# Token-stationary gate sums and projections in a hybrid diffusion trunk layer

## Chip, core and metric

The kernel runs on one core of one Trainium2 chip. The time is device microseconds of one execution, as the median of several runs. TensorE (PE) multiplies, VectorE (DVE) and ScalarE (ACT) do elementwise work, SyncE (SP) issues most transfers. Each of these works through its own queue in order, and a wait at the head holds what is behind it.

## What is computed

One trunk layer is applied to 128 context tokens and 256 latent tokens, 384 tokens in all (`TOK`), with `D_MODEL` 2048. Everything is float32. The part that matters here is `token_mixing`, between the input projection and the feed-forward part:

```python
def token_mixing(h, attn, u, w_na_proj, w_fnet_proj, w_gate, w_o):
    b, t = h.shape[:2]
    na = attn.reshape(b, t, D_NA) @ w_na_proj
    fn = fourier_mix(u) @ w_fnet_proj
    g_na, g_fn = jnp.split(jax.nn.sigmoid(h @ w_gate), 2, axis=-1)
    return (g_na * na + g_fn * fn) @ w_o
...
x = x + g1 * token_mixing(h, attn, u, ...)
h2 = rms_norm(x, n2) * (1 + sc2) + sh2
x = x + g2 * swiglu(h2, w_gu_l, w_down_l)
```

`h` is the normed and modulated input, `attn` the attention's output (1024 wide), `fourier_mix(u)` the real part of a 2-D DFT (1024 wide). `w_gate` is 2048 x 4096, the two projections 1024 x 2048 each, `w_o` 2048 x 2048.

## The kernel before

**Products.** A float32 product is made of three matmuls in a reduced format, `mm3` (L146 to L149): each operand is split into a high part H, cast by ScalarE (L143), and a low part L, the rest, by VectorE (L144). The first two operands of `mm3` (aH, aL) stand in the array as stationary operand, the last two (bH, bL) move through it. The stationary operand is 128 x 128; the moving one here has 384 or 512 columns. So there are two ways to do a product. With the tokens standing and 512 weight columns moving, the result has tokens on the partitions; w_in, w_o and w_down are done so (3 blocks of 128 tokens x 2 rows of the contraction x 3 = 18 matmuls a unit). With a 128 x 128 block of weights standing and 384 tokens moving, the result has channels on the partitions, as the next product's contraction needs them; the gate sums, the projections and w_gate_up are done so (4 blocks of 128 columns x 2 x 3 = 24 matmuls a unit).

**Weights.** All weights pass in units of 256 rows x 512 columns, in one list (`units`): w_in, w_gate (64 units), the two projections in turns of four units (32), w_o (32), then the feed-forward weights. A unit is loaded on SP's queue (L187) into one of four `wraw` buffers, split into one of three `wh` and `wl` buffers by `split_unit`, and used. `next_unit` sets the order: it splits a unit two ahead of the one it hands out, then gives each background piece its steps, then issues the next load.

**Background pieces.** A background piece is a Python generator that a `Paced` object advances by so many steps for each unit; each step puts instructions into the queues behind what is there already. `rows` adds up the modulation rows of the second norm and the gates (VectorE, L329, loads on SP, L299) at about one step a unit. During the gate sums a second one, `branches`, holds the Fourier mix and then the attention, with steps at the head of a unit and once in its middle (`mid_unit`).

**Gate sums.** For each of eight column blocks of w_gate (`fc8`), eight units of matmuls add into four PSUM tiles of 128 channels x 384 tokens. They are copied out (`gst`, L1033) by VectorE or ScalarE and stored to DRAM (`s_gate`, L1036) by ScalarE's queue.

**Projections and mix.** For each of four column blocks (`f4`), the stored gates are loaded (`load_gates`, three tiles `gl`), the sigmoid is taken, and four units of w_fnet_proj and then four of w_na_proj are multiplied; each result is multiplied into its gate tile (L1094). The mix of the block (`mixed`) is a background piece with two steps a unit: add the two gated parts (L1069), split the sum into `mixH` and `mixL`, which lie channels first, as w_o's contraction wants them. After the last block, everything in the background but `rows` is drained at once, and w_o begins (`for cc in range(4)`, L1168 on): tokens standing, sixteen k-tiles of the mix, residual and gain added at the end of each `cc`.

Of the kernel before, what the change touches and what calls it, by code (L numbers as in the profile page):

```python
# [13 lines left out]
F32 = mybir.dt.float32  # L14
# [5 lines left out]
P = 128  # L20
D = 2048
KT = D // P
# [7 lines left out]
TOK = CTX + LAT  # L30
NT = TOK // P
EPS = 1e-6
CH = 512
# [19 lines left out]
def fr(ap):  # L53

    return ap.bitcast(F32)
# [46 lines left out]
def trunk_kernel(ctx: ExitStack, tc: tile.TileContext, io: dict):  # L102
    nc = tc.nc
# [27 lines left out]
    dram = ctx.enter_context(tc.tile_pool(name="dram", bufs=1, space=DRAM))  # L131
# [6 lines left out]
    def nm(s):  # L138
        return f"{s}{next(ids)}"


    def split(H, L, x):
        nc.scalar.copy(H, x)  # L143
        nc.vector.tensor_sub(L, x, fr(H))  # L144

    def mm3(out, aH, aL, bH, bL, start, stop):  # L146
        nc.tensor.matmul(out, aH, bH, start=start, stop=False)  # L147
        nc.tensor.matmul(out, aH, bL, start=False, stop=False)  # L148
        nc.tensor.matmul(out, aL, bH, start=False, stop=stop)  # L149
# [45 lines left out]
    def split_unit():  # L195
        if loads.got:
            _, raw = loads.take()
            H = wpool.tile([P, 2, CH], F32R, tag="wh", name=nm("wh"))
            L = wpool.tile([P, 2, CH], F32R, tag="wl", name=nm("wl"))
            n = raw.shape[1]  # L200
            split(H[:, :n], L[:, :n], raw)
            ready.append((H, L))

    def mid_unit():
        for p in front:
            p.tick()

    def next_unit():

        for p in front:  # L210
            p.tick()
        split_unit()
        for p in front + behind:
            p.tick()
        loads.more()
        return ready.popleft()
# [12 lines left out]
    hH = [None] * KT  # L229
    hL = [None] * KT  # L230

    def new_h(kt):
        hH[kt] = hpool.tile([P, TOK], F32R, tag=f"tH{kt}", name=nm(f"hH{kt}_"))
        hL[kt] = hpool.tile([P, TOK], F32R, tag=f"tL{kt}", name=nm(f"hL{kt}_"))
        return hH[kt], hL[kt]

    s_qkvu = [dram.tile([P, NT, CH], F32, tag=f"sq{i}", name=f"s_qkvu{i}") for i in range(8)]
    s_gate = [dram.tile([P, 4, TOK], F32, tag=f"sg{i}", name=f"s_gate{i}") for i in range(8)]
    s_row = {
        ty: [dram.tile([1, D], F32, tag=f"row{ty}{c}", name=f"s_row{ty}{c}") for c in range(2)] for ty in (2, 3, 4, 5)  # L240
    }
# [24 lines left out]
    with ExitStack() as ph:  # L266
# [3 lines left out]
        def mm_tile():  # L270
            return ps.tile([P, CH], F32, tag="mm", name=nm("mm"))
# [6 lines left out]
        def new_ring(n=0):  # L278

            nonlocal ring  # L280
            ring = itertools.cycle([mm_tile] * n + [at_tile] * 3 + [mm_tile] * (4 - n))

        def acc_tile():

            return next(ring)()
# [152 lines left out]
        with ExitStack() as pha:  # L438
# [4 lines left out]
            def c6(shape, name):  # L443
                return cpool.tile(shape, F32, tag="c6", name=nm(name))
# [8 lines left out]
            for cc in range(4):  # L453
                t = c6([P, NT, CH], "xc")
# [195 lines left out]
            for gi, (k0, n) in enumerate(GROUPS):  # L650
# [5 lines left out]
                for rate, ci in zip(CHUNKS, ORDER):  # L656
                    if gi == len(GROUPS) - 1:
                        rows.rate = rate
                    po = [(mm_tile if gi < len(GROUPS) - 1 else acc_tile)() for _ in range(NT)]
                    if gi == 0:  # L660
                        acc[ci] = c6([P, NT, CH], "acc")
                    for u in range(k0, k0 + n, 2):
                        wH, wL = next_unit()
                        while prepared[0] < min(u + 2, k0 + n):
                            prep.step()
                        for t in range(NT):
                            sl = slice(t * P, (t + 1) * P)
# [5 lines left out]
                            if u + 2 >= k0 + n:  # L673
                                a = acc[ci][:, t]
# [15 lines left out]
        gst = ph.enter_context(tc.tile_pool(name="gst", bufs=4))  # L690
# [126 lines left out]
        soft = deque(maxlen=3)  # L817
# [197 lines left out]
        front += [br_work, rows]  # L1015
        behind.remove(rows)
        for fc8 in range(8):
            po = [mm_tile() for _ in range(4)]
            sts = []
            for u in range(0, KT, 2):  # L1020
                ending[0] = u == KT - 2
                rows.least = 3 if ending[0] else 1
                wH, wL = next_unit()
                for f in range(4):
                    s = slice(f * P, (f + 1) * P)
                    if f == 2:
                        mid_unit()
                    for kk in range(2):
                        k = u + kk
                        mm3(po[f][:, :TOK], wH[:, kk, s], wL[:, kk, s], hH[k], hL[k], k == 0, k == KT - 1)  # L1030
                    if u == KT - 2:
                        st = gst.tile([P, TOK], F32, tag="st", name=nm("gst"))
                        (nc.vector.tensor_copy if f < 2 and any(soft) else nc.scalar.copy)(st, po[f][:, :TOK])  # L1033
                        sts.append(st)
            for f, st in enumerate(sts):
                nc.scalar.dma_start(s_gate[fc8][:, f], st)  # L1036
        br_work.drain()
        rows.least = 1
        front.clear()
# [4 lines left out]
        bs = ph.enter_context(tc.tile_pool(name="bsplit", bufs=1))  # L1044
# [8 lines left out]
                yield  # L1053

        def load_gates(f4, i):
            g = bs.tile([P, 4, TOK], F32, tag="gl", bufs=3, name=nm("gl"))
            nc.sync.dma_start(g, s_gate[i * 4 + f4])
            return g

# [2 lines left out]
        gates = Ahead(load_gates, [(f4, i) for f4 in range(4) for i in (1, 0)], 3)  # L1062
        mixH, mixL = [None] * KT, [None] * KT

        def mixed(f4, gl):
            for f in range(4):
                kt = f4 * 4 + f
                mixH[kt], mixL[kt] = new_h(kt)
                nc.vector.tensor_add(gl[0][:, f], gl[0][:, f], gl[1][:, f])  # L1069
                split(mixH[kt], mixL[kt], gl[0][:, f])  # L1070
                if f == 3:
                    yield
                    gates.more()
                    gates.more()
                yield

        new_ring(1)
        for f4 in range(4):
            gl = [None, None]
            for i, bH, bL in ((1, fH, fL), (0, aH, aL)):  # L1080
                _, gl[i] = gates.take()
                po = [acc_tile() for _ in range(4)]
                for u in range(0, 8, 2):
                    wH, wL = next_unit()
                    if u == 4:
                        nc.scalar.activation(out=gl[i], in_=gl[i], func=AF.Sigmoid)
                    for f in range(4):
                        s = slice(f * P, (f + 1) * P)
                        for kk in range(2):
                            k = u + kk  # L1090
                            mm3(po[f][:, :TOK], wH[:, kk, s], wL[:, kk, s], bH[k], bL[k], k == 0, k == 7)
                        if u < 6:
                            continue
                        nc.vector.tensor_mul(gl[i][:, f], gl[i][:, f], po[f][:, :TOK])  # L1094
            behind.append(Paced(mixed(f4, gl), 2))
        behind.remove(rows)
        for p in behind:
            p.drain()
# [69 lines left out]
    for cc in range(4):  # L1168
        xin[cc] = tmp.tile([P, NT, CH], F32, tag="xin", name=nm("xin"))
        behind.append(Paced(load_residual(cc)))  # L1170
        po = [acc_tile() for _ in range(NT)]
        for u in range(0, KT, 2):
            if cc == 3 and u == KT - 4:
                rows.rate = 0
            if cc == 3 and u == 8:
                warm_sqrt()
            wH, wL = next_unit()
            if cc == 3 and u == KT - 2:
                rows_until(3)
                shifts(xw, 0)  # L1180
            if u == 2 and cc:
                rows_until(4)
                behind.append(Paced(transposed(cc - 1), 0.5))
            for t in range(NT):
                sl = slice(t * P, (t + 1) * P)
                for kk in range(2):
                    k = u + kk
                    mm3(po[t], mixH[k][:, sl], mixL[k][:, sl], wH[:, kk], wL[:, kk], k == 0, k == KT - 1)
                if u == KT - 2:
                    d = tmp.tile([P, CH], F32, tag="d", name=nm("d"))  # L1190
                    nc.vector.tensor_mul(d, po[t], gb[cc][:, min(t, 1)])
                    nc.vector.tensor_add(x2[cc][:, t], xin[cc][:, t], d)
                    junk = tmpo.tile([P, CH], F32, tag="junk", name=nm("junk"))
                    nc.scalar.activation(
                        out=junk, in_=x2[cc][:, t], func=AF.Square, accum_out=ssx[:, t, cc : cc + 1]
                    )
# [96 lines left out]
    for part, nf in enumerate(FF_PARTS):  # L1293
# [5 lines left out]
        for c4 in range(nf // 4):  # L1299
            for half in (1, 0):  # L1300
                po = [acc_tile() for _ in range(4)]
                bs = []
                for u in range(0, KT, 2):
                    wH, wL = next_unit()
                    for f in range(4):
                        s = slice(f * P, (f + 1) * P)
                        for kk in range(2):
                            k = u + kk
# [6 lines left out]
                        if half and f == 0:  # L1315
                            sg = tmp.tile([P, 4, TOK], F32, tag="xin", name=nm("sg"))
# [20 lines left out]
        for cc in range(4):  # L1337
            po = [acc_tile() for _ in range(NT)]
            for u in range(0, nf, 2):
                wH, wL = next_unit()  # L1340
                for t in range(NT):
                    sl = slice(t * P, (t + 1) * P)
                    for kk in range(2):
                        k = u + kk
# [66 lines left out]
```

## Time and profile before

| | |
|---|---|
| median of three runs | 2045.47 us (2044.15 to 2046.48) |
| profiled execution, span | 2046.3 us |
| PE busy | 2023.5 us, 99% |
| weight loads into PE (PEld) | 1843.5 us, 90% |
| VectorE busy | 1260.9 us, 62% |
| ScalarE busy | 741.1 us, 36% |
| gate sums, first to last load of w_gate | 314.9 to 640.1 us |
| projections, first to last load | 643.6 to 782.9 us |
| w_o, first to last load | 789.0 to 916.9 us |

The span is from the first to the last instruction of the profiled execution; the profile gives no separate time for what lies around it. Busy time of an engine is the union of its instructions, whose durations overlap on TensorE, so a TensorE that shows as fully busy says little of how close its matmuls follow each other; the starts in the timeline say that. L12 is line 12 of the kernel. In a group, "out<-in" names what is written and read, then the number of instructions, their busy time and mean ns, and the idle time ahead of them with what ended it. DMA issues have the time from issue to landing. Loads are issued some units ahead of use, so the stretches in the table are those of the loads.

### The profile page before, as it was taken

What the parts mean: (1) busy time and instruction counts of PE and PEld (TensorE: products, weight loads), DVE (VectorE), ACT (ScalarE), POOL (GpSimd) and SP (SyncE); (2) the same over time, 40 slices, a digit from 0 to 9 for tenths busy, and PEclk for the clock granted to TensorE, in tenths of its full rate; (3) what the DMA queues carried; (4) which work ended last, traced back from release to release, by engine and by line L of the source; (5) the groups of instructions that cost most, each with busy time, mean ns of one, the idle gap of its engine ahead of it and who ended that gap; (6) DMA issues with size and microseconds to landing.
All of it is one profiled execution on the core that took longest, in us unless ns stands there. A gap on an engine that the chain in (4) does not pass through costs nothing.

```text
span 2046.3 us, 27564 instructions
## 1 busy us (share of the span) xinstructions
PE 2023.5 (99%) x10986; PEld 1843.5 (90%) x10986; DVE 1260.9 (62%) x1578; ACT 741.1 (36%) x1093; POOL 43.7 (2%) x92
## 2 busy tenths in 40 slices
PE   7999999999999999999999999999999999999999
PEld 4668888999999999889998999899989998999897
DVE  4646989789988778755845454545454334333456
ACT  4433232445555443334523332322322232323222
POOL 1000000000010000010000000000000000000000
PEclk8999999999999999999999999999999999999999
DMA  9995979677775776754455555554554444444453
GB/s 309 335 343 187 321 258 324 217 232 224 231 204 177 250 253 190 247 182 144 119 174 156 153 155 156 150 157 146 160 158 138 124 130 125 132 124 124 138 161 124
DMA packets 220384, 390.46 MB, mean 191 GB/s; under 512 B 28464, under 2 KB 77632, under 8 KB 220256
## 3 DMA queue, kind: packets, MB, share of 16 engines
q1 hardware_dynamic: 213088, 382.13, 59.7%
q10 hardware_dynamic: 4672, 6.31, 0.8%
q8 instruction: 86, 1.41, 0.3%
q0 software_dynamic: 2496, 0.27, 0.1%
q14 instruction: 42, 0.34, 0.0%
HBM read 371.81 MB, written 20.51 MB: 192 GB/s over the span
## 4 chain that ended last, share of the span: by engine, by line
PE 96%; DMA 2%; DVE 1%; ACT 0%; SPq 0%; issue 0%; DVEq 0%
PE mm L147 20%; PE mm L149 19%; PE mm L148 19%; PE at L147 11%; PE at L149 11%; PE at L148 11%; PE at L405 1%; DMA wm<-in_w_mod 1%; DMA wraw<-in_w_in 1%; PE at L978 1%; PE at L957 1%; DMA xc<-in_x_prompt 1%; PE at L894 1%; DVE wl L144 0%; PE at L338 0%; PE at L1154 0%
## 5 line engine op out<-in xcount | busy, mean ns | idle before, releaser
L144 DVE TENSOR_TENSOR wl<-wraw,wh 128x1024 fp32r<-128x1024 f32 (+1 forms) x464 | 559.3, 1206 | 683.8 <-ACT wh L143 683.6
L143 ACT CAST wh<-wraw 128x1024 fp32r<-128x1024 f32 (+1 forms) x464 | 481.1, 1038 | 1086.9 <-PE at L148 273.9
L147 PE MATMUL mm<-hH,wh 128*128 128x384 f32 x1152 | 387.7, 337 | 0.0
L149 PE MATMUL mm<-hH,wl 128*128 128x384 f32 x1152 | 385.2, 334 | 0.0
L148 PE MATMUL mm<-hL,wh 128*128 128x384 f32 x1152 | 385.1, 334 | 0.0
L329 DVE SCALAR_TENSOR_TENSOR accr<-wmr,csz,accr 128x1024 f32<-128x1024 f32 x240 | 304.2, 1280 | 0.1
L147 PEld LDWEIGHTS mm<-hH,wh 128*128 128x128 f32 x1152 | 216.2, 188 | 3.7 <-issue 3.7
L148 PEld LDWEIGHTS mm<-hL,wh 128*128 128x128 f32 x1152 | 216.3, 188 | 0.0
L149 PEld LDWEIGHTS mm<-hH,wl 128*128 128x128 f32 x1152 | 216.2, 188 | 0.0
L147 PE MATMUL at<-hH,wh 128*128 128x384 f32 x640 | 213.9, 334 | 0.0
L149 PE MATMUL at<-hH,wl 128*128 128x384 f32 x640 | 213.9, 334 | 0.0
L148 PE MATMUL at<-hL,wh 128*128 128x384 f32 x640 | 213.8, 334 | 0.0
L147 PE MATMUL mm<-wh,hH 128*128 128x512 f32 x404 | 160.8, 398 | 1.9 <-ACT hH L546 1.2
L148 PE MATMUL mm<-wl,hH 128*128 128x512 f32 x404 | 158.2, 392 | 0.8 <-DVE wl L144 0.8
L149 PE MATMUL mm<-wh,hL 128*128 128x512 f32 x404 | 158.5, 392 | 0.4 <-DVE hL L144 0.4
L147 PE MATMUL mm<-wh,cH 128*128 128x512 f32 x352 | 137.0, 389 | 0.0
L149 PE MATMUL mm<-wh,cL 128*128 128x512 f32 x352 | 137.0, 389 | 0.0
L148 PE MATMUL mm<-wl,cH 128*128 128x512 f32 x352 | 137.0, 389 | 0.0
L147 PEld LDWEIGHTS at<-hH,wh 128*128 128x128 f32 x640 | 120.1, 188 | 1.0 <-ACT wh L143 0.8
L148 PEld LDWEIGHTS at<-hL,wh 128*128 128x128 f32 x640 | 120.1, 188 | 0.2
L149 PEld LDWEIGHTS at<-hH,wl 128*128 128x128 f32 x640 | 120.1, 188 | 0.0
L147 PEld LDWEIGHTS mm<-wh,hH 128*128 128x128 f32 x404 | 76.2, 189 | 26.1 <-issue 4.4
(284 smaller groups left out, 2627.9 us busy)
## 6 DMA issues: line engine op xcount, KB each, us to landing
wraw<-in_w_gate_up SPq DMA_DIRECT2D x176, 512.0 KB, 3.7
wmr<-in_w_mod SPq DMA_DIRECT2D x128, 512.0 KB, 5.0
wraw<-in_w_down SPq DMA_DIRECT2D x88, 512.0 KB, 3.7
wraw<-in_w_gate SPq DMA_DIRECT2D x64, 512.0 KB, 4.6
wm<-in_w_mod SPq DMA_DIRECT2D x80, 384.0 KB, 6.8
wraw<-in_w_in SPq DMA_DIRECT2D x56, 512.0 KB, 5.9
wraw<-in_w_o SPq DMA_DIRECT2D x32, 512.0 KB, 4.7
wraw<-in_w_fnet_proj SPq DMA_DIRECT2D x16, 512.0 KB, 4.8
```

The source lines that it names most:

```text
L143: nc.scalar.copy(H, x)
L144: nc.vector.tensor_sub(L, x, fr(H))
L147: nc.tensor.matmul(out, aH, bH, start=start, stop=False)
L148: nc.tensor.matmul(out, aH, bL, start=False, stop=False)
L149: nc.tensor.matmul(out, aL, bH, start=False, stop=stop)
L329: nc.vector.scalar_tensor_tensor(out=acc[:, cnd], in0=wm, scalar=sc, in1=acc[:, cnd], op0=ALU.mult, op1=ALU.add)
L405: nc.tensor.matmul(pm[q : q + 32, :w], csz[:, k, :], wm[:, ty, kk + par, :], start=k < 2, stop=k >= KT - 2, tile_position=(0, q), skip_gro ...
L894: nc.tensor.matmul(po[j][:, cols], qx[rows[j], q], kx[rows[j], k], start=i == 0, stop=i == 2, tile_position=(j * HD, 0),)
L957: nc.tensor.transpose(o[:, i * P : (i + 1) * P], sc[:, j, c0 : c0 + P], ident)
L978: nc.tensor.matmul(po[j][:, CTX:TOK].rearrange("p (t q) -> p t q", t=2), w[1 + kc], x.rearrange("p (t b) q -> p t b q", t=2)[:, :, 2 * kc ...
```

## The change

Gate sums and projections take the other way: tokens standing, 512 weight columns moving, 18 matmuls a unit. The gate sums come out with tokens on the partitions, in three PSUM tiles of 128 tokens x 512 channels, are copied out by three copies (the first by VectorE when attention's step allows it, the others by ScalarE) and stored as three transfers; the DRAM buffer has the shape `[P, NT, CH]`. The middle step of a unit stands in the middle of its 18 matmuls. The projections multiply into gate tiles of the same shape.

The mix therefore has tokens on the partitions and has to be turned for w_o. `mixed` adds the two parts in three additions, transposes the sum with three instructions on VectorE, in blocks of 32 x 32, from the first gate tile into the second, and moves the blocks between partitions with 16 transfers from SBUF to SBUF on SP's queue, back into the first gate tile; each moves 32 partitions x 4 pieces of 96 numbers. The splits then read the turned tile. The steps of `mixed`, two a unit: two additions; the third addition, the transposes and the transfers; an empty step; the load of a gate tile and the first split; three steps with a split each; the load of another gate tile.

Since w_o's first eight k-tiles come from the first two blocks, its first four units are multiplied straight after the projections, ahead of the drain, into `out_po`; the first `cc` goes on from there.

```diff
-    s_gate = [dram.tile([P, 4, TOK], F32, tag=f"sg{i}", name=f"s_gate{i}") for i in range(8)]
+    s_gate = [dram.tile([P, NT, CH], F32, tag=f"sg{i}", name=f"s_gate{i}") for i in range(8)]
...
         for fc8 in range(8):
-            po = [mm_tile() for _ in range(4)]
+            po = [mm_tile() for _ in range(NT)]
...
-                for f in range(4):
-                    s = slice(f * P, (f + 1) * P)
-                    if f == 2:
-                        mid_unit()
+                for t in range(NT):
+                    sl = slice(t * P, (t + 1) * P)
                     for kk in range(2):
                         k = u + kk
-                        mm3(po[f][:, :TOK], wH[:, kk, s], wL[:, kk, s], hH[k], hL[k], k == 0, k == KT - 1)
+                        if t == 1 and kk:
+                            mid_unit()
+                        mm3(po[t], hH[k][:, sl], hL[k][:, sl], wH[:, kk], wL[:, kk], k == 0, k == KT - 1)
                     if u == KT - 2:
-                        st = gst.tile([P, TOK], F32, tag="st", name=nm("gst"))
-                        (nc.vector.tensor_copy if f < 2 and any(soft) else nc.scalar.copy)(st, po[f][:, :TOK])
+                        st = gst.tile([P, CH], F32, tag="st", name=nm("gst"))
+                        (nc.vector.tensor_copy if t < 1 and any(soft) else nc.scalar.copy)(st, po[t])
                         sts.append(st)
-            for f, st in enumerate(sts):
-                nc.scalar.dma_start(s_gate[fc8][:, f], st)
+            for t, st in enumerate(sts):
+                nc.scalar.dma_start(s_gate[fc8][:, t], st)
...
         def mixed(f4, gl):
+            raw, tr = (
+                g.rearrange("p t n -> p (t n)").rearrange("p (a k t r) -> p a k t r", a=4, k=4, t=NT) for g in gl
+            )
+            for t in range(NT):
+                nc.vector.tensor_add(gl[0][:, t], gl[0][:, t], gl[1][:, t])
+                if t == 1:
+                    yield
+            for t in range(NT):
+                nc.vector.transpose(
+                    tr[:, :, :, t].rearrange("p g k r -> p k g r"),
+                    gl[0][:, t].rearrange("p (k g r) -> p k g r", k=4, g=4),
+                )
+            for i in range(4):
+                for g in range(4):
+                    nc.sync.dma_start(raw[32 * g : 32 * g + 32, :, i], tr[32 * i : 32 * i + 32, g])
+            yield
+            yield
+            gates.more()
             for f in range(4):
                 kt = f4 * 4 + f
                 mixH[kt], mixL[kt] = new_h(kt)
-                nc.vector.tensor_add(gl[0][:, f], gl[0][:, f], gl[1][:, f])
-                split(mixH[kt], mixL[kt], gl[0][:, f])
-                if f == 3:
-                    yield
-                    gates.more()
-                    gates.more()
+                split(
+                    *(x.rearrange("p (t i r) -> p t i r", t=NT, r=32) for x in (mixH[kt], mixL[kt])),
+                    raw[:, f].rearrange("p i t r -> p t i r"),
+                )
                 yield
+            gates.more()
...
-                    for f in range(4):
-                        s = slice(f * P, (f + 1) * P)
+                    for t in range(NT):
+                        sl = slice(t * P, (t + 1) * P)
                         for kk in range(2):
                             k = u + kk
-                            mm3(po[f][:, :TOK], wH[:, kk, s], wL[:, kk, s], bH[k], bL[k], k == 0, k == 7)
+                            mm3(po[t], bH[k][:, sl], bL[k][:, sl], wH[:, kk], wL[:, kk], k == 0, k == 7)
                         if u < 6:
                             continue
-                        nc.vector.tensor_mul(gl[i][:, f], gl[i][:, f], po[f][:, :TOK])
+                        nc.vector.tensor_mul(gl[i][:, t], gl[i][:, t], po[t])
             behind.append(Paced(mixed(f4, gl), 2))
+        out_po = [acc_tile() for _ in range(NT)]
+        for u in range(0, 8, 2):
+            wH, wL = next_unit()
+            for t in range(NT):
+                sl = slice(t * P, (t + 1) * P)
+                for kk in range(2):
+                    k = u + kk
+                    mm3(out_po[t], mixH[k][:, sl], mixL[k][:, sl], wH[:, kk], wL[:, kk], k == 0, False)
         behind.remove(rows)
         for p in behind:
             p.drain()
...
-        po = [acc_tile() for _ in range(NT)]
-        for u in range(0, KT, 2):
+        po = [acc_tile() for _ in range(NT)] if cc else out_po
+        for u in range(0 if cc else 8, KT, 2):
```

More of the change, by code (lines that the diff above doesn't have):

```diff
@@ L1055, in load_gates @@
         def load_gates(f4, i):
-            g = bs.tile([P, 4, TOK], F32, tag="gl", bufs=3, name=nm("gl"))
+            g = bs.tile([P, NT, CH], F32, tag="gl", bufs=3, name=nm("gl"))
             nc.sync.dma_start(g, s_gate[i * 4 + f4])
@@ L1081, in trunk_kernel @@
                 _, gl[i] = gates.take()
-                po = [acc_tile() for _ in range(4)]
+                po = [acc_tile() for _ in range(NT)]
                 for u in range(0, 8, 2):
```

## The prediction, written before the result was known

> **What bounds the kernel now.** First the page: shares of the engines and the chain of work that ended last.
>
> ```profile
> span 2046.3 us, 27564 instructions
> PE 2023.5 (99%) x10986; PEld 1843.5 (90%) x10986; DVE 1260.9 (62%) x1578; ACT 741.1 (36%) x1093; POOL 43.7 (2%) x92
> PE 96%; DMA 2%; DVE 1%; ACT 0%; SPq 0%; issue 0%; DVEq 0%
> ```
>
> TensorE sets the end: it is 96% of the chain. The time can fall only if its instructions come closer together, and rises by whatever makes it wait. So the second view is the timeline of TensorE, where starts count, not durations (the 0.33 us of neighbouring matmuls overlap). Two stretches without other work, first and last row of each: 18 steps with 384 columns moving, 27 steps with 512.
>
> ```profile
> 689.86 0.33 PE L147 MATMUL mm<-aH,wh 128*128 128x384 f32 x1
> ...
> 692.98 0.33 PE L147 MATMUL mm<-aH,wh 128*128 128x384 f32 x1
> ```
> ```profile
> 1499.74 0.39 PE L147 MATMUL mm<-wh,cH 128*128 128x512 f32 x1
> ...
> 1505.86 0.39 PE L147 MATMUL at<-wh,cH 128*128 128x512 f32 x1
> ```
>
> 3.12/18 = 0.1733 us a step at 384, 6.12/27 = 0.2267 us at 512. The difference, 0.0533 us for 128 columns, leaves 0.1733 - 3 x 0.0533 = 0.013 us that a matmul costs whatever its width. TensorE is bound by columns, with a small fixed part.
>
> The third view is busy time by stretch: 50 us of the gate sums, then the second and fourth of the four projection groups (PE, PEld, DVE, ACT, POOL; then clock, DMA share, GB/s).
>
> ```profile
> 500.00:550.00 50.00, 50.00 (x323) 49.37 (x323) 47.80 (x72) 28.72 (x63) 0.00 (x0) 1.00 0.78 231
> 706.40:740.00 33.60, 33.60 (x196) 33.60 (x195) 28.35 (x35) 13.11 (x15) 0.00 (x0) 1.00 0.74 247
> 773.00:806.50 33.50, 33.50 (x195) 33.50 (x194) 28.26 (x35) 12.91 (x14) 0.00 (x0) 1.00 0.68 213
> ```
>
> VectorE is at 96% in the gate sums and 84% in the projections, so a wait in its queue is not easily caught up. What runs in the projections, by groups:
>
> ```profile
> L329 DVE SCALAR_TENSOR_TENSOR accr<-wmr,csz,accr 128x1024 f32<-128x1024 f32 x31 | 39.3, 1280 | 0.0
> L144 DVE TENSOR_TENSOR wl<-wraw,wh 128x1024 fp32r<-128x1024 f32 x30 | 36.7, 1224 | 18.8 <-ACT wh L143 18.8
> L1069 DVE TENSOR_TENSOR gl<-gl,gl 128x384 f32<-128x384 f32 x12 | 6.6, 553 | 0.0
> L344 DVE TENSOR_TENSOR row<-row,accr 128x512 f32<-128x512 f32 x1 | 0.7, 684 | 0.0
> L143 ACT CAST wh<-wraw 128x1024 fp32r<-128x1024 f32 x31 | 32.5, 1051 | 46.4 <-PE at L148 26.1 <-PE mm L148 14.4 <-issue 5.8
> L143 ACT CAST hH<-gl 128x384 fp32r<-128x384 f32 x12 | 6.2, 515 | 24.6 <-DVE gl L1069 24.6
> ```
>
> The fifth row is the one to keep: ScalarE's cast of the weights (wh) waits for TensorE, since wh has three buffers. The cast made during unit n is for unit n+2, so it has two units to be late in, and no more.
>
> **The matmuls.** A unit was 24 matmuls at 384 and becomes 18 at 512: 24 x 0.1733 = 4.160 us against 18 x 0.2267 = 4.080 us, 0.08 us less. Gate sums have 64 units, projections 32: 96 x 0.08 = -7.7 us (-5.1 and -2.6). The columns are the same; only the fixed part of six matmuls a unit goes. Other PE work, the weight loads from HBM and the sigmoids stay. Stores of the gate sums go from four issues to three, and copies out of PSUM from four of 384 to three of 512, the same elements: nothing, covered by an ACT that is 57% busy there (28.72 of 50).
>
> The Trainium skill speaks against even this gain: "TensorE: Matmul & The Clock Gate", section Back-to-back issue gap, gives N/2.4 + 2.5 ns for a matmul. By it the fixed part is 2.5 ns, and six matmuls in 96 units are worth 1.4 us, an estimate from that page; the rows above differ from it and decide.
>
> **The boundary to w_o.** Today the last mix is drained in one piece before the first w_o unit, and the weights queue behind it; the next two rows are VectorE's and TensorE's timelines there.
>
> ```profile
> 814.65 1.23 DVE L144 TENSOR_TENSOR wl<-wraw,wh 128x1024 fp32r<-128x1024 f32 x1 [0.40 <-ACT wh L143]
> ```
> ```profile
> 815.93 0.50 PE L148 MATMUL mm<-wl,hH 128*128 128x512 f32 x1 [0.76 <-DVE wl L144]
> ```
>
> With four w_o units ahead of the drain that goes: -0.8 us. The loads of the first residual and its gains (gb) are issued four units later: the last one in the unit of u = 12, where VectorE wants it some 6 us later, and it takes 5.0 us (among the landing times quoted below). If it is late, VectorE waits a us or two once, which the two units of lead hide: nothing.
>
> **The mix on VectorE.** Per group of eight units: products 3 of 512 for 4 of 384, additions likewise (0.68 for 0.55 us each: 4.1 against 4.4 in all), the four splits as before, and three new block transposes of 512 columns. The trace has none. Bounds: a 512 column operation with one input cannot well be dearer than twice the 0.68 us of one with two, and I take the nearest, 0.6 us (a step; neighbours overlap by 0.08). VectorE gets 1.5 us more in 33, and reaches 91%: no bound of its own while nothing waits. For the price the Trainium skill alone has a figure: "VectorE: DVE Perf Modes", The three transpose paths, 311 ns for 128x128 bf16, four times 1.24 us as an estimate; by it the first transfer starts 1.9 us later and the sum grows by 7.7 us.
>
> **The transfers, and who waits.** Each group now has 16 SBUF transfers on SP's queue, 32 partitions with pieces of 384 B. They wait for the third transpose. All 16 must land before any split, since each writes 32 partitions of every k-tile. The splits stand in ScalarE's and VectorE's queues ahead of the weights of later units. So I follow one group in time, from T, the end of the previous group's matmuls. How VectorE gets to the first addition is seen after the group that ended at T = 738.77 (ScalarE's row, then VectorE's):
>
> ```profile
> 738.77 1.05 ACT L143 CAST wh<-wraw 128x1024 fp32r<-128x1024 f32 x1 [3.10 <-PE at L148]
> ```
> ```profile
> 739.89 1.22 DVE L144 TENSOR_TENSOR wl<-wraw,wh 128x1024 fp32r<-128x1024 f32 x1
> 741.02 1.28 DVE L329 SCALAR_TENSOR_TENSOR accr<-wmr,csz,accr 128x1024 f32<-128x1024 f32 x1
> 742.22 0.56 DVE L1069 TENSOR_TENSOR gl<-gl,gl 128x384 f32<-128x384 f32 x1
> ```
>
> First addition at T + 3.45, three at 0.6: 5.25, three transposes at 0.6: 7.05. Then SP. What issues back to back cost there, small pieces (L823 to L825, L844) and whole rows (L187, L299):
>
> ```profile
> 580.53 0.55 SPq L823 DMA_DIRECT2D qp<-s_qkvu  x1
> 581.17 0.57 SPq L824 DMA_DIRECT2D kp<-s_qkvu  x1
> 581.79 0.60 SPq L825 DMA_DIRECT2D kp<-in_cache_k  x1
> 582.49 0.39 SPq L187 DMA_DIRECT2D wraw<-in_w_gate  x1
> 582.92 0.46 SPq L299 DMA_DIRECT2D wmr<-in_w_mod  x1
> ```
> ```profile
> gb<-s_row SPq DMA_DIRECT2D x16, 256.0 KB, 5.0
> ...
> bp<-s_rpb SPq DMA_DIRECT2D x32, 96.0 KB, 5.3
> ...
> out_y_sample<-x SPq DMA_DIRECT2D x8, 256.0 KB, 2.1
> ...
> vp<-in_cache_v SPq DMA_DIRECT2D x8, 64.0 KB, 3.4
> ```
>
> A step is (582.49 - 580.53)/3 = 0.65 us for small pieces, 0.43 us (582.92 - 582.49) for whole rows. Mine are small pieces: I take 0.65 and keep 0.43 as the low end. The 16th issue starts at 7.05 + 15 x 0.65 = 16.8. Landing, from the issue rows just shown: 2.1 us in an empty queue, 5.3 us for the smallest pieces, and 3.4 us for the 64 KB load that is nearest to 48 KB; I take 3.4. **All have landed at T + 20.2.**
>
> ScalarE reaches the first split in unit 1 of the new group (the mix has two steps a unit; addition to transfers are steps 1 and 2, the split is step 4) and stands there from about T + 5.2. Queued behind it: the cast of unit 4's weights, then VectorE's wl for them. They end 0.44 + 0.97 + 1.15 = 2.6 us after the landing (515, 1051 and 1224 ns, less the overlap of 0.08): T + 22.8. TensorE wants this wl in the second matmul of unit 4, T + 4 x 4.08 + 0.23 = T + 16.55. **It waits 6.2 us.** After that, unit 5's weights: the second and third split, the sigmoid and the cast follow on ScalarE, some 3.5 us, while unit 4 runs 4.08: no further wait. SP is late too: the weight load behind the 16 issues leaves at T + 17.5, is wanted by a cast after T + 22, and lands in that 4 to 5 us; no price.
>
> This happens after each of four groups, after the last one in w_o's first units, where the new code has the same order: 4 x 6.2 = +24.8 us.
>
> **Sum.** -7.7 - 0.8 + 24.8 = +16.3. The profiled execution: 2046.3 + 16.3 = 2062.6; its span is 0.8 us over the median of the runs, 2045.47, and its time outside the span isn't shown, so I take that 0.8 off: 2062. Bounds of the same sum: whole-row issues and the empty queue give a landing at 7.05 + 6.45 + 2.1 = 15.6, a wait of 1.65 us, and -1.9 us in all: 2043.6. Transposes at twice the price and the slow landing give 7.05 + 1.8 + 9.75 + 5.3 = 23.9, a wait of 9.95 us, +31.3: 2077.
>
> **Rivals.** *The transfers are hidden* (other side): if they land by T + 13.95, ScalarE isn't late and all that is left is -8.5: 2037. It becomes a gain from a landing before T + 16.1 on. For it: SBUF to SBUF has no HBM at either end, and no such transfer is in the trace. Against it: 16 issues at the cheapest step seen already take 6.45 us after the transposes, which leaves 0.45 us to land. *Cheap transfers*: the low bound above, 2044, no change. *The clock falls in the waits*: while TensorE had little to do early on, the granted clock fell to half for several us (windows; the clock is third from the end).
>
> ```profile
> 20.00:24.00 4.00, 2.80 (x67) 2.12 (x67) 2.14 (x7) 0.57 (x2) 0.00 (x0) 1.00 0.79 239
> 24.00:28.00 4.00, 2.03 (x6) 1.33 (x7) 2.88 (x8) 1.91 (x5) 0.00 (x0) 0.72 0.93 295
> 28.00:32.00 4.00, 4.00 (x19) 2.08 (x21) 1.76 (x3) 1.59 (x3) 0.00 (x0) 0.50 1.01 348
> ```
>
> The lost clock in these rows is 4 x 0.28 + 4 x 0.5 = 3.1 us. If each of the four waits of 6 us brings that, 2062 + 12 = 2074. Against it: a wait of 6 us may be too short, and VectorE is behind just then, so part is hidden. The Trainium skill's rule on this ("TensorE: Matmul & The Clock Gate", Part 1) is that an idle window of about 3.4 us halves the clock until a busy one has passed; the trace agrees that idle time brings half the clock, and no row shows how much of it suffices. *VectorE bounds the gate sums*: at 47.80 of 50 it could hold the stage, and 5.1 us of gain are lost: 2067, inside the range.
>
> **Chances.** Forecast with its VectorE variant 0.44; hidden transfers 0.16; cheap transfers 0.16; clock 0.20; worse than all of these 0.04. The range 2042 to 2079 holds the second bound, the clock and the cheap case, and leaves out the hidden case and the worst, 0.20. A measurement of this kernel can't tell less than 0.2% (4.1 us) from no change: faster 0.16 (hidden), same 0.16 (cheap), slower 0.68.
>
> **What would show it.** Right: matmuls of the gate sums and projections at steps of 0.227 us; four waits of TensorE of some 6 us, each at the fifth unit after a group, released by ScalarE's or VectorE's weights, with ScalarE idle ahead of the split cast (hH) until a transfer lands; SP issuing 16 transfers in about 10 us. Wrong: the split cast idle under 2 us, or a landing before T + 14; transposes well off 0.6 us; TensorE's step above 0.23 us. If the waits are longer with the clock at half behind them, the third rival holds.

## The result and the profile after

| | before | changed |
|---|---|---|
| median of four runs | 2045.02 us (2044.15 to 2046.48) | 2070.03 us (2069.29 to 2071.16) |
| profiled span | 2046.3 us | 2069.3 us |

The change makes the kernel slower: ratio 1.0121, 95% interval 1.0107 to 1.0136, that is 25 us. The page of the changed kernel:

```profile
span 2069.3 us, 26460 instructions
PE 2027.1 (98%) x10410; PEld 1775.1 (86%) x10410; DVE 1265.8 (61%) x1575; ACT 740.7 (36%) x1088; POOL 43.7 (2%) x92
PE 88%; DVE 5%; DMA 3%; SPq 2%; issue 1%; ACT 1%; ACTq 0%; DVEq 0%
```

TensorE has 576 matmuls fewer and is no longer 96% of the chain but 88%; VectorE, transfers and SP's queue are on it now. Where the time lies is read from the first loads of each stage, before and after (each row: the shortest, median and longest issue in ns, then the start of the first and of the last load of that weight).

```profile
L187 SPq DMA_DIRECT2D wraw<-in_w_gate x64: 367/378/1413, 314.9 to 640.1; - x64
L187 SPq DMA_DIRECT2D wraw<-in_w_fnet_proj x16: 367/378/385, 643.6 to 763.1; - x16
L187 SPq DMA_DIRECT2D wraw<-in_w_gate_up x176: 367/368/384, 920.8 to 1981.9; - x176
```
```profile
L187 SPq DMA_DIRECT2D wraw<-in_w_gate x64: 367/378/1485, 315.6 to 636.1; - x64
L187 SPq DMA_DIRECT2D wraw<-in_w_fnet_proj x16: 367/373/548, 639.6 to 772.9; - x16
L187 SPq DMA_DIRECT2D wraw<-in_w_gate_up x176: 367/368/384, 943.8 to 2004.8; - x176
```

From the first load of w_gate to that of w_fnet_proj it was 328.7 us and is 324.0: the gate sums gain 4.7. From there to the first load of w_gate_up it was 277.2 us and is 304.2: projections and w_o lose 27.0. After that the distance to the last load is the same, 1061.1 and 1061.0 us.

The loss is four waits of TensorE and a slow clock around them. Its timeline at the first one (start, duration, in brackets the idle time and what ended it), then ScalarE's and SP's there; the group before ended with the matmuls at T = 700.7, the T of the prediction:

```profile
716.81 0.39 PE L149 MATMUL at<-wh,fL 128*128 128x512 f32 x1
721.85 0.80 PE L147 MATMUL at<-wh,aH 128*128 128x512 f32 x1 [4.65 <-ACT wh L143]
723.11 0.79 PE L148 MATMUL at<-wl,aH 128*128 128x512 f32 x1 [0.47 <-DVE wl L144]
723.70 0.63 PE L149 MATMUL at<-wh,aL 128*128 128x512 f32 x1
724.13 0.63 PE L147 MATMUL at<-wh,aH 128*128 128x512 f32 x1
```
```profile
705.00 1.06 ACT L143 CAST wh<-wraw 128x1024 fp32r<-128x1024 f32 x1 [3.02 <-PE at L149]
720.33 0.51 ACT L143 CAST hH<-gl 128x384 fp32r<-128x384 f32 x1 [14.28 <-DMA gl<-gl]
720.75 1.04 ACT L143 CAST wh<-wraw 128x1024 fp32r<-128x1024 f32 x1
```
```profile
708.24 10.40 SPq L1080 DMA_DIRECT2D gl<-gl  x16
718.74 0.54 SPq L187 DMA_DIRECT2D wraw<-in_w_na_proj  x1
```

The 16 transfers take SP 10.40 us to issue; the first split (hH) stands in ScalarE's queue for 14.28 us until the last has landed; the cast of the weights (wh) stands behind it, and TensorE, which should have gone on at 717.04, gets its first matmul at 721.85 and the second at 723.11. Against steps of 0.227 us that is 4.8 + 1.0 = 5.8 us lost. The other three groups lose 4.3, 6.8 and 6.4 us by the same count: 23.3 us.

The last two rows of TensorE stand 0.43 us apart, not 0.227: the clock. Busy time around the wait, with the granted clock third from the end:

```profile
700.00:717.00 17.00, 17.00 (x76) 13.89 (x75) 10.48 (x14) 2.11 (x2) 0.00 (x0) 1.00 0.35 96
717.00:721.80 4.80, 0.20 (x1) 0.00 (x0) 0.56 (x1) 1.47 (x3) 0.00 (x0) 0.73 0.53 136
721.80:726.00 4.20, 3.69 (x8) 2.60 (x9) 4.17 (x5) 4.20 (x6) 0.00 (x0) 0.50 0.83 302
726.00:740.00 14.00, 14.00 (x64) 11.56 (x62) 14.00 (x15) 4.87 (x5) 0.00 (x0) 1.00 0.96 347
```

The last 4.2 us at half clock lie behind the wait. Matmuls that took such slow steps lost 6.8 us over the four groups.

### The profile page after: what moved, and what is told of

The parts are those of the page before. It is cut to its first block, busy times and chain, and to the rows that moved or that the text cites. A ratio compares the mean times of both kernels' runs of the same rounds, so it can differ in the third digit from the quotient of the medians.

```text
span 2069.3 us, 26460 instructions
## 1 busy us (share of the span) xinstructions
PE 2027.1 (98%) x10410; PEld 1775.1 (86%) x10410; DVE 1265.8 (61%) x1575; ACT 740.7 (36%) x1088; POOL 43.7 (2%) x92
## 4 chain that ended last, share of the span: by engine, by line
PE 88%; DVE 5%; DMA 3%; SPq 2%; issue 1%; ACT 1%; ACTq 0%; DVEq 0%
PE mm L147 18%; PE mm L148 17%; PE mm L149 17%; PE at L148 11%; PE at L147 11%; PE at L149 11%; SPq L1080 2%; DVE accr L329 1%; DVE wl L144 1%; DMA wm<-in_w_mod 1%; PE at L405 1%; ACT wh L143 1%; PE at L978 1%; PE at L957 0%; DMA xc<-in_x_prompt 0%
## 5 line engine op out<-in xcount | busy, mean ns | idle before, releaser
L147 PE MATMUL mm<-wh,hH 128*128 128x512 f32 x788 | 313.8, 398 | 1.9 <-ACT hH L546 1.2
L149 PE MATMUL mm<-wh,hL 128*128 128x512 f32 x788 | 308.9, 392 | 0.7 <-DVE hL L144 0.4
L148 PE MATMUL mm<-wl,hH 128*128 128x512 f32 x788 | 308.5, 391 | 0.0
L147 PE MATMUL mm<-hH,wh 128*128 128x384 f32 x640 | 213.9, 334 | 0.0
L148 PE MATMUL mm<-hL,wh 128*128 128x384 f32 x640 | 213.8, 334 | 0.0
L149 PE MATMUL mm<-hH,wl 128*128 128x384 f32 x640 | 213.8, 334 | 0.0
L149 PEld LDWEIGHTS mm<-wh,hL 128*128 128x128 f32 x788 | 148.8, 189 | 33.7 <-DVE hL L144 1.1
L148 PEld LDWEIGHTS mm<-wl,hH 128*128 128x128 f32 x788 | 148.9, 189 | 28.9
L147 PEld LDWEIGHTS mm<-hH,wh 128*128 128x128 f32 x640 | 120.1, 188 | 0.8 <-ACT wh L143 0.8
L148 PEld LDWEIGHTS mm<-hL,wh 128*128 128x128 f32 x640 | 120.1, 188 | 0.0
```

## The experiments

The expectations weigh three theories of the loss. A: the first split waits at the head of ScalarE's queue for the transfers, and the casts of the weights wait behind it. B: the work that VectorE has been given in addition is the cost. C: A holds, and even a short wait halves the clock.

Each ratio is against the kernel before in the same series of runs, with medians between 2044.85 and 2045.77 us. Ahead of the first load of w_gate, where all these kernels are the same, the traces differ by up to 4.4 us (312.5 to 316.9), so stretches between loads say more than whole spans.

**The transfers left out.**

```diff
-            for i in range(4):
-                for g in range(4):
-                    nc.sync.dma_start(raw[32 * g : 32 * g + 32, :, i], tr[32 * i : 32 * i + 32, g])
```

> The 64 transfers from SBUF to SBUF are left out, so the splits read the mix unturned; additions, transposes and the place of the splits stay as in the changed kernel. A: nothing for ScalarE to wait for, 2036.5 us. B: VectorE's work is all still there: 2060 or more.

Measured: 2037.93 us, ratio 0.9967 (0.9954 to 0.9980). TensorE shows no wait between 640 and 860 us in this trace, and the stage rows are these:

```profile
L187 SPq DMA_DIRECT2D wraw<-in_w_fnet_proj x16: 367/373/426, 636.9 to 754.7; - x16
L187 SPq DMA_DIRECT2D wraw<-in_w_gate_up x176: 367/368/384, 910.5 to 1971.4; - x176
```

Projections and w_o take 273.6 us, 3.6 less than before and 30.6 less than in the changed kernel; 23.3 of waits and 6.8 at the slow clock account for 30.1 of these. All of VectorE's added work is in this kernel, so theory B, that this work is the cost, falls. The transfers, and what waits for them, cost 32 us (2070.03 - 2037.93), and the rest of the change gains 7 (2044.85 - 2037.93). The result of this kernel is not that of the layer, since the blocks stay where they are.

**Only the gate sums.** The gate part of the diff alone, with this load:

```diff
...
+            nc.sync.dma_start(g, s_gate[i * 4 + f4].rearrange("p t n -> p (t n)").rearrange("p (f m) -> p f m", f=4))
```

> Only the gate sums are done with tokens standing and 512 columns moving; projections, mix and w_o are those of the kernel before, and read the stored gates in the wrong order. If the fixed part of a matmul is the gain: 64 units x 0.08 = 5.1 us less, 2040 us. If VectorE bounds this stage (47.80 of 50 us busy): 2045 us.

Measured: 2041.48 us, 0.9983 (0.9974 to 0.9992): 3.4 us less, 1.6 to 5.3 by the interval.

```profile
L187 SPq DMA_DIRECT2D wraw<-in_w_gate x64: 367/379/1527, 315.2 to 635.1; - x64
L187 SPq DMA_DIRECT2D wraw<-in_w_fnet_proj x16: 367/378/395, 638.6 to 758.0; - x16
```

From load to load the gate sums take 323.4 us against 328.7, 5.3 less, near the 5.1 worked out from the fixed part of a matmul. VectorE does not bound them.

**The split later.** Empty steps, two to a unit, ahead of the first split (n = 2 and n = 4):

```diff
             gates.more()
+            for _ in range(n):
+                yield
             for f in range(4):
```

> The mix's first split stands two steps, that is one unit (4.08 us), later in the queues; transfers, additions and transposes stay where they are. Theory A (the split cast waits at the head of ScalarE's queue and the weights wait behind it): each of TensorE's four waits, 23 us in all in the changed kernel, gets 4.08 us shorter, some 7 us are left; the clock no longer falls behind such short waits: 2044 us. Theory B (VectorE's added work is the cost): nothing changes, 2070. Theory C (also a short wait halves the clock): four times 2 us more than A, 2052.

> The same with four steps, two units. A: the split cast still waits for the last transfer (landing at some 19.6 us after the group), for some 6 us, but what stands behind it is wanted two units later: no wait of TensorE, clock at full rate, 2045 - 8.5 = 2036.5 us. B: 2070. C: as A, since there is no wait.

Measured: 2058.49 us (1.0063, 1.0048 to 1.0078) and 2054.90 us (1.0044, 1.0028 to 1.0061). One unit later takes away 11.5 us, so the place of the split counts, as theory A says; but 2044 and 2036.5 were expected, and the second unit brings only 3.6 us more, with intervals that overlap. What A's sum left out with two steps stands in ScalarE's queue, here in the first group:

```profile
716.68 0.51 ACT L143 CAST hH<-gl 128x384 fp32r<-128x384 f32 x1 [10.10 <-DMA gl<-gl]
717.10 1.48 ACT L1105 ACTIVATE gl<-gl 128x1536 f32<-128x1536 f32 x1
718.48 1.03 ACT L143 CAST wh<-wraw 128x1024 fp32r<-128x1024 f32 x1
```

The split is now followed by the sigmoid of a gate tile, 1.4 us ahead of the weights; in the changed kernel the weights came next. With it, A's sum gives 19.5 + 1.4 + 2.6 - (16.55 + 4.08) = 2.9 us here, and 3.0 were measured. With four steps the split is out of the way in the first three groups, and something else ends the waits. (After the last group the four splits are drained together, still ahead of w_o's weights; 3.3 us are lost there.) ScalarE, with four steps, in the second group:

```profile
757.16 0.51 ACT L143 CAST hH<-gl 128x384 fp32r<-128x384 f32 x1 [9.54 <-DMA gl<-gl]
761.30 1.04 ACT L143 CAST wh<-wraw 128x1024 fp32r<-128x1024 f32 x1 [3.62 <-DMA wraw<-in_w_na_proj]
```

The cast now waits 3.62 us for the weights themselves. SP's queue in the same run, in the first group:

```profile
705.42 10.38 SPq L1080 DMA_DIRECT2D gl<-gl  x16
715.90 0.54 SPq L187 DMA_DIRECT2D wraw<-in_w_na_proj  x1
717.33 0.34 SPq L1057 DMA_DIRECT2D gl<-s_gate  x1
717.73 0.43 SPq L187 DMA_DIRECT2D wraw<-in_w_na_proj  x1
718.20 0.46 SPq L299 DMA_DIRECT2D wmr<-in_w_mod  x1
718.70 1.73 SPq L187 DMA_DIRECT2D wraw<-in_w_fnet_proj  x2
```

For 10.4 us no weight load can leave; then four of them, a gate tile and a modulation load leave within 5 us, and in the 6 us after that the DMA engines are 98% busy. So theory A alone falls, and a second one stands beside it: D, the same transfers hold the weight loads behind them on SP's queue. In the changed kernel the wait at ScalarE covered it. Theory C was right in part: with two steps TensorE's wait in the first group is 2.0 us for wh and 1.0 for wl, and the clock falls there too, while with four steps it does not after 1.6 + 1.0 us (third group). The length of the wait does not decide alone, as a run below shows. 5.6 us are lost to slow steps with two steps, against 6.8 in the changed kernel.

**The weight load first.** The kernel with four steps, and in projections and w_o's first units each unit's load issued ahead of the background steps (`turning[0]` is set there and nowhere else):

```diff
...
         split_unit()
+        if turning[0]:
+            loads.more()
         for p in front + behind:
             p.tick()
-        loads.more()
+        if not turning[0]:
+            loads.more()
```

> All 16 transfers on SP's queue and the first split two units later, as in the run with four more steps; but in projections and w_o's first units each unit's weight load is issued ahead of the background steps, so one load goes before the 16 transfers instead of behind them. D (late weight loads, and their burst after the transfers, are what is left in that run): the load of unit 6 leaves at 3.5 us after the group instead of 18, each later one comes a place earlier, and a load issued at 18 lands before its cast at 20.4 to 22: the waits are gone, 2038 to 2041 us. If the loads' lateness is not the cause: 2055 as in that run.

Measured: 2045.66 us, 1.0003 (0.9994 to 1.0013). One place in SP's queue is worth 9.2 us, with the same transfers and the same splits: D holds. In the traces TensorE's waits after the first three groups fall from 8.8 to 2.5 us, and no half clock follows them any more. 2038 to 2041 was not reached. TensorE still waits 6.1 us, and not for late weights in the main: the 2.5 us come from VectorE, where the low half of the split, and then three products, stand ahead of wl; 2.0 are the splits drained together after the last group; 1.5 come at the end of w_o's first `cc`, where VectorE waits for the gains (gb). ScalarE's waits for weight loads between 640 and 860 us (total, times, longest), with four steps and then with the load first:

```profile
ACT wh L143 <- DMA wraw<-in_w_na_proj: 13.9, 5, 3.7
...
ACT wh L143 <- DMA wraw<-in_w_fnet_proj: 5.5, 3, 2.7
...
ACT wh L143 <- DMA wraw<-in_w_o: 4.6, 4, 1.9
```
```profile
ACT wh L143 <- DMA wraw<-in_w_fnet_proj: 7.1, 3, 3.9
...
ACT wh L143 <- DMA wraw<-in_w_na_proj: 1.7, 3, 0.9
```

24.0 us have become 9.9, 1.1 of it for w_o's loads.

**Another queue.** All transfers and the gate loads on GpSimd's queue:

```diff
-            nc.sync.dma_start(g, s_gate[i * 4 + f4])
+            nc.gpsimd.dma_start(g, s_gate[i * 4 + f4])
...
-                    nc.sync.dma_start(raw[32 * g : 32 * g + 32, :, i], tr[32 * i : 32 * i + 32, g])
+                    nc.gpsimd.dma_start(raw[32 * g : 32 * g + 32, :, i], tr[32 * i : 32 * i + 32, g])
```

> The 16 transfers of each mix and the loads of the gate tiles are issued on GpSimd's queue instead of SP's; the splits stand where the changed kernel has them. A step there was 0.48 us in the kernel before, so the last transfer lands at 7.5 + 15 x 0.48 + 2.0 = 16.7 us after the group. Theory A alone (ScalarE's queue): the split cast still holds the weights behind it, a wait of 16.7 + 2.6 - 16.55 = 2.8 us in each of four groups: 2037.9 + 11 = 2049, some us more where the clock falls. Theory D (the weight loads behind the transfers on SP's queue) alone: SP is free, 2038.

> Transfers and gate loads on GpSimd's queue, and the first split two units later. A and D together: no queue that feeds TensorE waits for a transfer, so the time is that of the kernel without transfers, 2038 us, faster than the kernel before. If a third thing waits (VectorE's load, the transfers' share of the DMA engines): 2045 or more.

Measured: 2071.99 us (1.0132, 1.0117 to 1.0147) and, with four steps more ahead of the split, 2060.85 us (1.0075, 1.0058 to 1.0092). The first missed by over 20 us, and the second came out under its last case, 2045 or more. The landing was not at 16.7, but at 19.9 us after the first group: GpSimd's timeline in the first of the two shows why.

```profile
707.55 4.92 POOL L1080 DMA_DIRECT2D gl<-gl  x9 [41.77 <-issue]
712.94 1.09 POOL L1080 DMA_DIRECT2D gl<-gl  x2 [0.47 <-DMA gl<-gl]
715.07 2.86 POOL L1080 DMA_DIRECT2D gl<-gl  x5 [1.04 <-DMA gl<-gl]
```

After nine issues it waits for earlier transfers to land. On SP's queue, which carries no weight load meanwhile, a transfer landed in 2.0 us (median); here, beside the weight loads that SP now sends, in 3.4, and in the second run in 5.8:

```profile
gl<-gl SPq DMA_DIRECT2D x64, 48.0 KB, 2.0
```
```profile
gl<-gl POOLq DMA_DIRECT2D x64, 48.0 KB, 5.8
```

With the landing as late as before, the split waits as long as before, and A gives the changed kernel's time again. In the second run the last transfer lands 23.3 us after the first group, so that the split is late even two units further on. Neither run tells A from D by itself. The trace of the second also bears on theory C: in its second group TensorE loses 0.8 + 2.4 us, and the granted clock stays at 1.00.

**Half on each queue.** Eight transfers on SP's queue, eight on GpSimd's, gate loads on GpSimd's; the split one unit later, then where the changed kernel has it:

```diff
...
+                    (nc.sync if g % 2 else nc.gpsimd).dma_start(raw[32 * g : 32 * g + 32, :, i], tr[32 * i : 32 * i + 32, g])
```

> Half the transfers on SP's queue, half on GpSimd's, gate loads on GpSimd's, the first split one unit later. The last lands at 7.5 + 7 x 0.65 + 2.0 = 14 us after the group; the split cast stands from 9 us on, the weights behind it are wanted at 20.6: no wait on that side. The weight load on SP leaves at 12.8 instead of 18: A and D give 2038 us; if eight issues still make a load late, 2042.

> As the run with half the transfers on GpSimd's queue, but the splits stand where the changed kernel has them, one unit earlier. The transfers land at 14.4 us after the group there. A (ScalarE's queue): the weights behind the split are ready at 14.4 + 2.6 = 17.0 and wanted at 16.55, a wait of 0.45 us in each of four groups: 2042 us. If the place of the splits decided, and not when the transfers land: 2050 or more.

Measured: 2039.87 us (0.9974, 0.9963 to 0.9984), **faster than the kernel before** with the whole change in it; and 2046.15 us (1.0002, 0.9992 to 1.0011). In the faster one SP is held for 5.25 us and the split's wait is covered; TensorE shows no wait for weights in these stages, and projections and w_o take 914.8 - 640.8 = 274.0 us, for 273.6 without transfers:

```profile
709.40 5.25 SPq L1080 DMA_DIRECT2D gl<-gl  x8
```
```profile
716.30 0.51 ACT L143 CAST hH<-gl 128x384 fp32r<-128x384 f32 x1 [5.05 <-DMA gl<-gl]
```
```profile
L187 SPq DMA_DIRECT2D wraw<-in_w_fnet_proj x16: 367/368/424, 640.8 to 762.0; - x16
L187 SPq DMA_DIRECT2D wraw<-in_w_gate_up x176: 367/368/384, 914.8 to 1975.7; - x176
```

The same run settles one thing on GpSimd's queue: with half of the transfers there they land in 2.2 us, and in 2.3 on SP's. The queue as such is not the slower one.

```profile
gl<-gl POOLq DMA_DIRECT2D x32, 48.0 KB, 2.2
```

With the split a unit earlier the waits are back: 6.3 us in the trace, where the same stretch takes 281.1 us. The medians differ by 6.3 too (2046.15 - 2039.87), by 5.6 if each is taken against the median of its own series. 1.8 us of waits were expected, from the landing in one group, 14.4. The split cast starts 14.6, 16.0, 15.8 and 16.2 us after the four groups; by A's sum that makes 0.6, 2.1, 1.9 and 2.3 us, and TensorE waits 0.8, 1.0, 2.0 and 2.5. So A's sum holds with the landings that came about, but for the second group. After the second and third group the transposes end 8.8 and 8.7 us behind the group, after the first 7.5: two modulation steps fall into the unit ahead of the additions after the third, where it was one after the first. After the fourth they end at 7.6, and it is the transfers that take longer.

```profile
768.84 2.47 DVE L329 SCALAR_TENSOR_TENSOR accr<-wmr,csz,accr 128x1024 f32<-128x1024 f32 x2
771.23 1.88 DVE L1070 TENSOR_TENSOR gl<-gl,gl 128x512 f32<-128x512 f32 x3
773.15 1.90 DVE L1074 STREAM_TRANSPOSE gl<-gl 128x512 f32<-128x512 f32 x3
```

So VectorE's queue decides a little too, by when the transfers may start, but not alone.

**Without w_o's first units.** As the faster one, but the last mix is drained in one piece, as before the change:

```diff
-        out_po = [acc_tile() for _ in range(NT)]
-        for u in range(0, 8, 2):
...
-        po = [acc_tile() for _ in range(NT)] if cc else out_po
-        for u in range(0 if cc else 8, KT, 2):
+        po = [acc_tile() for _ in range(NT)]
+        for u in range(0, KT, 2):
```

> As the run with half the transfers on GpSimd's queue and the splits one unit later, but w_o's first four units are not put ahead of the drain: the last mix is drained in one piece as in the kernel before. A: after the last group the four splits wait for the transfers (14.4 us), the weights of w_o's third unit are cast behind them, ready at 14.4 + 4 x 0.44 + 0.97 + 1.15 = 18.3 us and wanted at 8.4: one wait of 9.9 us and some 2 us at half clock, 2040 + 12 = 2052 us. If the units ahead of the drain hide nothing: 2040.

Measured: 2051.56 us (1.0029, 1.0019 to 1.0038), 11.7 us more than with the units ahead of the drain. TensorE at that place:

```profile
813.09 0.80 PE L147 MATMUL at<-wh,hH 128*128 128x512 f32 x1 [7.87 <-ACT wh L143]
814.35 0.80 PE L148 MATMUL at<-wl,hH 128*128 128x512 f32 x1 [0.46 <-DVE wl L144]
```

One wait, about where A puts it, and half clock after it. The part of the change that moves w_o's first units does what it says.

**Both.** Half on each queue, the split one unit later, and the load first:

> The run with half the transfers on GpSimd's queue and the splits one unit later, with the weight load of a unit issued ahead of the background steps as well. That run had no wait of TensorE left in its trace, so there is nothing more to win on this side: the time without transfers, 2038 us, is the floor; 2038 to 2040 us by A and D. Higher, if the load order itself costs something (a modulation load, now behind the weight load, late for VectorE).

Measured: 2041.47 us (0.9980, 0.9971 to 0.9989), no better than without the new order; its interval overlaps that of the faster kernel above. Its trace has 2.2 us of waits. Where SP is held for 5 us only, the place of the load is worth nothing that shows.

## Why the prediction was right, and where it was short

Forecast was a rise of 16.3 us, to 2062; the span grew by 23.0, the median by 25. That lies between the forecast and the third rival (2074), and by the prediction's own sign, half clock behind the waits, it is the rival that holds, at about half its price. The path of the wait was right. Point by point:

- *The matmuls*, -7.7, with -0.8 at the boundary: right. The gate sums gained 4.7 us (5.3 alone) for 5.1, projections and boundary 3.6 for 3.4 (without the transfers). The steps are 0.227 us. The N/2.4 + 2.5 ns that the prediction sets against this gain is, in the Trainium skill ("TensorE: Matmul & The Clock Gate", Back-to-back issue gap), the gap of an isolated matmul. The matmuls here come in a stream, each with its weight load, and the 13 ns held. The count of VectorE's products left out one of the two projections: 6.1 us against 6.6 instead of 4.1 against 4.4, without effect.
- *The transposes*: three took 1.90 us in the timeline with 0.684 us each, so 0.61 us a step for the 0.6 taken. The 1.24 us that was worked out from the Trainium skill's figure ("VectorE: DVE Perf Modes", The three transpose paths) is twice what this trace shows.

```profile
L1074 DVE STREAM_TRANSPOSE gl<-gl 128x512 f32<-128x512 f32 x12 | 7.6, 684 | 0.1
```

- *The transfers on SP*: 16 issues in 10.40 us, 0.65 a step, as taken from other small pieces. The landing after the issue took 2.0 us, not 3.4. First transfer at T + 7.5 for 7.05, split at T + 19.6 for 20.2: two errors against each other, and some luck in how near the sum came.
- *The wait*: 5.8 us in the first group, 23.3 in all four, for 6.2 and 24.8. The four are 5.8, 4.3, 6.8 and 6.4, so one price for all held on the average only. Right, and the mechanism with it: first split at the head of ScalarE's queue, weights behind it.
- *The clock*: here the sum was short. The fall to half clock stood among the rivals at 12 us and 0.20; it came after each wait, and 6.8 us of slow steps are as much as separates 16.3 from 23.0. They are less than 12, since part of the half clock falls into the wait itself: in the first group it begins at 719.2, and TensorE goes on at 721.85. The argument against it, that 6 us may be too short, was wrong: it came after 2.0 + 1.0 us as well, though not after 1.6 + 1.0, and in another run not after 0.8 + 2.4. The page's rule (the Trainium skill, "TensorE: Matmul & The Clock Gate", Part 1) asks for an idle window of some 3.4 us; the waits of 5.8 us here agree with it, and the one of 3.0 us shows that a little less, with a single matmul in it, was enough in this kernel, but not each time.
- *SP's late load, "no price"*: right for the changed kernel, where the other wait covers it (one cast waited 4.0 us for its load, after the third group, and TensorE did not), and wrong as a statement on the queue. As soon as the split is out of the way it is the next wait, worth 9 us for one place.
- *The hidden-transfer rival* needed a landing before T + 16.1 for a gain. With half the transfers on each queue and a split one unit later it came about, and the gain followed. That landing alone was not enough: with the split in its old place the transfers landed 14.5 to 15.7 us after the groups, and the time was that of before.

What stays open: of the span's 23.0 us, -4.7 - 3.6 + 23.3 + 6.8 = 21.8 are accounted for; of the other 1.2, 0.7 lie ahead of the first load of w_gate (315.6 against 314.9), outside the change; the medians' 25 can't be split further. Why 16 transfers on GpSimd's queue take up to three times as long, and eight do not, was seen, not taken apart: their number or the weight loads beside them. And what decides, among waits of about 3 us, whether the clock falls was not tested.

## What to carry to other kernels

A turn through transfers is cheap in engine time and dear in queues: ask of each queue that issues or waits for a transfer what stands behind it, and by when that is wanted, and when one wait is moved away, look for the next queue that the same transfers hold. An operation that waits for a transfer belongs as many units behind it in its queue as the transfer takes, in the kernel that came out faster two, at 4.08 us each; and what newly comes to stand between it and the weights, such as a sigmoid, counts as well. The gain of wider moving operands is the fixed part of the matmuls saved, here 0.013 us apiece, so a stall of a few us undoes hundreds of them, the more so as the clock falls in it.

## What had not been expected of the hardware

At half clock matmuls stood 0.43 us apart for 4.2 us after a wait of 5.8; waits of 3.0 us brought the half clock too, one of 2.6 and one of 3.2 did not. In these stages the half clock lasted 3.4, 6.8 or 10.2 us, and within a trace its stretches begin whole multiples of 3.41 us apart (in the changed kernel at 719.2, 763.5, 801.1 and 842.1), which suggests that it matters where a wait falls, and not only how long it is. Transfers of 48 KB from SBUF to SBUF landed in 2.0 us while SP sent nothing else and in 3.4 to 5.8 us (medians) when all 16 of a mix went through GpSimd's queue, with weight loads beside them; that queue stopped after nine issues until earlier ones had landed. With eight on each queue it was 2.2 and 2.3 us.
